# A hybrid attention and Fourier encoder layer on one core: where the meta rows' sums are stored, where the last sums of a weight are made, and which cast comes first in the merge

## The chip, the cores and the metric

The kernel runs on one core of one Trainium2 chip. The core has a matrix engine (TensorE, PE in the profile, with its weight loads as PEld), a vector engine (VectorE, DVE), a scalar engine (ScalarE, ACT), a general engine (GpSimd, POOL) and an engine that only issues transfers (SyncE, SP). Each works through its own list of instructions in order, and semaphores tie the lists together. Transfers between the main memory (HBM) and the on-chip memory (SBUF) run on 16 DMA engines; a transfer is issued from the list of one engine, here from SP's or POOL's. TensorE writes into eight banks of a separate memory, PSUM. The metric is the device time of one execution in microseconds (us); lower is better.

## The reference, cut to what matters

Two request groups go through one layer with the same weights: a sample of 512 positions and a prompt of 1024. Sixteen learned meta tokens stand in front of each. For the change these lines matter:

```python
x = jnp.concatenate([meta, x], axis=1)                       # 16 meta rows first
h = rmsnorm(x, g_mix)
q, k, v, u, gate_na, gate_fn = split(h @ w_in)
y_na = neighbourhood_attention(q, k, v, rel_bias, meta_bias) @ w_branch_na
f = jnp.fft.fft2(u, axes=(positions, group channels), norm='ortho').real
y_fn = f @ w_branch_fn
mixed = sigmoid(gate_na) * y_na + sigmoid(gate_fn) * y_fn
x = x + mixed @ w_out
a = relu(rmsnorm(x, g_mlp) @ w_up)
x = x + (a * a) @ w_down
y = rmsnorm(x, g_final)[16:]                                 # meta rows dropped
```

All arithmetic is float32.

## The kernel before, in words

**Numbers in two parts.** Every operand of a matmul is held as a high part (a rounded copy, cast by ScalarE, `L152` or `L133`) and a low part (the rest, subtracted by POOL or VectorE, `L153` or `L134`). A product is three matmuls (`mm3`, L129): high by high, high by low, low by high. A weight tile thus costs a load into a raw buffer, a cast and a subtraction (`weights`, L146 to L156) before TensorE can use it. The raw buffers of `wtile` are two, so the third weight of a stream is loaded when the first has been subtracted.

**Order.** The sample goes first through the whole layer up to the MLP, then the prompt, which takes the down projection of both. The kernel is traced as one long program; a planner in the compiler orders each engine's list by the order of the trace and by estimated times. The kernel holds it back by hand in two ways: `behind(marks)` puts every instruction of a block behind given instructions of the same engine, and `pinned()` puts it behind the last instruction that has been traced on each engine. So what is pinned keeps its place in the list of its engine, and a transfer that waits holds up everything behind it on SP.

**The sample's stages around the change.**
- `project_v` (L306 on) makes the values and stores them; it also sees the normed, transposed activations `hT` with the meta columns in front, and runs once with `meta is None`, for the sample.
- `gates` (L774 on) makes the two sigmoid gates of eight blocks `dm`, 24 matmuls each. Between its steps it advances two generators: `fold_u`, and then `fold_positions` (L863 on), the latter eight times. A step of `fold_positions` adds high and low parts of `hT` into a buffer `a` (for the sample one buffer, the tile `gain` of pool `mlp`) and into another `b`, stores the first 16 columns of `a` to `hmeta` in HBM (L885), and folds `a` and `b` onto each other (L886 to L888). `hmeta` is read once, by the prompt (L411).
- `merge_na` (L808 on) multiplies the attention's output with W_na and the gate. It is behind the marks of `gates` at `dm == 5`. Its weights are loaded at L813 into the tile `relu`.
- `fn_ahead` (L835 on) is a generator. W_fn is needed as eight tiles, each the sum or difference of two inputs A and B (L845, two VectorE instructions a tile, called a sum below; there are eight sums). A goes into one of four buffers `raw`, B into one of the two halves of `gain`. The result is stored to HBM for the prompt (L847, `wfn`), and the first four are split at once into high and low parts. One call makes the sum of the tile asked for in the call before, and asks for the next tile (L853).
- `fourier_channels` (L955 on) is the transform over channels, in two parts of three position tiles. After each tile it calls `fn_ahead`, pinned: twice in part 0 and once in part 1 (L1000). With one call at the end of `merge_na` that makes ten, where nine are needed.
- `fourier_positions` (L1016 on) is the transform over positions. It needs the high and low parts of `uc` and `us` that the stage before has made; it ends on VectorE with L1054 and L1055.
- `merge_fn` (L903 on) multiplies with W_fn, gates and adds: on VectorE L938 (times the gate) and L939 (plus the attention's part) for each `dm`. After each second `dm` the pair is split, ScalarE L945 and VectorE L946, two instructions each. Behind this, pinned, a W_out tile is loaded, cast and subtracted (`out_weights`, L1059). The third W_out tile is subtracted by VectorE, the others by POOL.
- `project_out` (L1067 on) multiplies with W_out. Its first two products take the first three merged pairs and W_out tiles, and the fourth follows.

## Time and profile before

| | |
|---|---|
| three runs | 1954.2, 1959.82, 1959.96 us |
| their median | 1959.82 us |
| the profiled execution, its own time | 1960.86 us |
| its span, first to last instruction | 1959.0 us |
| mean granted clock of TensorE | 0.992 |
| TensorE busy | 1902.8 us, 97% |
| VectorE, ScalarE, GpSimd busy | 1151.1, 733.3, 815.0 us |
| mean rate of the transfers | 183 GB/s |

How to read it: the span is the time from the first to the last instruction of the one execution that was profiled, and the time of that execution is a little longer. A busy share is the share of the span in which an engine had an instruction under way; matmuls are pipelined, so a busy TensorE is not TensorE at its peak. The granted clock is the share of full speed that TensorE was given; it is shown for each stretch that one asks for. In a timeline a row stands for one instruction or for a run of like ones: start, duration, engine, line of the kernel, operation, output and input, shape, count, and in brackets how long the engine had been idle before and who ended that. The views are named in the prediction where their rows are shown.

### The profile page before, as it was taken

What the parts mean: (1) busy time and instruction counts of PE and PEld (TensorE: products, weight loads), DVE (VectorE), ACT (ScalarE), POOL (GpSimd) and SP (SyncE); (2) the same over time, 40 slices, a digit from 0 to 9 for tenths busy, and PEclk for the clock granted to TensorE, in tenths of its full rate; (3) what the DMA queues carried; (4) which work ended last, traced back from release to release, by engine and by line L of the source; (5) the groups of instructions that cost most, each with busy time, mean ns of one, the idle gap of its engine ahead of it and who ended that gap; (6) DMA issues with size and microseconds to landing.
All of it is one profiled execution on the core that took longest, in us unless ns stands there. A gap on an engine that the chain in (4) does not pass through costs nothing.

```text
span 1959.0 us, 26257 instructions
## 1 busy us (share of the span) xinstructions
PE 1902.8 (97%) x9435; PEld 1594.7 (81%) x9435; DVE 1151.1 (59%) x1916; ACT 733.3 (37%) x1292; POOL 815.0 (42%) x672
## 2 busy tenths in 40 slices
PE   7999999999999999999999999999999999999997
PEld 5888787888888888888898877888887888888886
DVE  6771744799625566660427475656665326758668
ACT  3664323344314556641223233333343323323333
POOL 1344535355521233333134217978882323323331
PEclk9999999999999999999999999999999999999999
DMA  6756873677756455374452432544446868558733
GB/s 218 198 146 214 220 224 97 201 246 252 248 191 186 124 153 144 113 238 113 114 158 81 172 97 86 183 172 160 174 163 238 293 213 291 205 202 303 260 103 124
DMA packets 313058, 358.39 MB, mean 183 GB/s; under 512 B 51880, under 2 KB 222504, under 8 KB 312376
## 3 DMA queue, kind: packets, MB, share of 16 engines
q1 hardware_dynamic: 295168, 334.93, 52.0%
q0 software_dynamic: 17760, 21.80, 4.9%
q8 instruction: 74, 1.21, 0.3%
q14 instruction: 56, 0.46, 0.1%
HBM read 263.06 MB, written 96.16 MB: 183 GB/s over the span
## 4 chain that ended last, share of the span: by engine, by line
PE 74%; DVE 8%; DMA 6%; issue 5%; POOL 3%; ACT 3%; SPq 1%; DVEq 0%; ACTq 0%; POOLq 0%
PE ps_mm L129 19%; PE ps_o L129 17%; PE ps_s L129 15%; PE ps_t L129 10%; PE ps_mm L522 3%; PE ps_mm L523 3%; PE ps_mm L524 3%; POOL w_lo L153 2%; PE ps_o L671 2%; PE ps_t L651 1%; DVE st L182 1%; DMA w_raw<-in_w_in 1%; DMA hmeta<-gain 1%; DMA w_raw<-in_w_out 1%; DVE h_lo L153 1%
## 5 line engine op out<-in xcount | busy, mean ns | idle before, releaser
L153 POOL TENSOR_TENSOR w_lo<-w_raw,w_hi 128x1024 fp32r<-128x1024 f32 x71 | 179.2, 2524 | 226.7 <-ACT w_hi L152 175.9
L153 POOL TENSOR_TENSOR w_lo<-raw,w_hi 128x1024 fp32r<-128x1024 f32 (+1 forms) x49 | 101.4, 2073 | 213.5 <-ACT w_hi L152 206.9
L152 ACT CAST w_hi<-w_raw 128x1024 fp32r<-128x1024 f32 x88 | 92.5, 1051 | 172.9 <-PE ps_s L129 48.9
L153 DVE TENSOR_TENSOR h_lo<-long,h_hi 128x1024 fp32r<-128x1024 f32 x54 | 84.6, 1569 | 79.1 <-ACT h_hi L152 79.1
L522 PE MATMUL ps_mm<-hT,w_hi 128*128 128x512 f32 (+2 forms) x296 | 122.0, 412 | 0.0
L523 PE MATMUL ps_mm<-hT,w_hi 128*128 128x512 f32 (+2 forms) x296 | 111.0, 375 | 0.0
L524 PE MATMUL ps_mm<-hT,w_lo 128*128 128x512 f32 (+2 forms) x296 | 110.9, 375 | 0.0
L152 ACT CAST h_hi<-long 128x1024 fp32r<-128x1024 f32 x54 | 56.7, 1050 | 106.6 <-issue 31.0
L153 DVE TENSOR_TENSOR hs_lo<-short,hs_hi 128x512 fp32r<-128x512 f32 x54 | 63.8, 1182 | 41.9 <-ACT hs_hi L152 41.8
L645 ACT ACTIVATE sc<-sc,ast 128x288 f32<-128x288 f32 (+4 forms) x96 | 53.9, 561 | 71.2 <-DVE ast L643 71.0
L1380 POOL TENSOR_TENSOR x<-w_hi,x 128x512 fp32r<-128x512 f32 (+1 forms) x42 | 70.9, 1688 | 16.3 <-ACT x L1383 16.3
L152 ACT CAST w_hi<-raw 128x1024 fp32r<-128x1024 f32 (+1 forms) x49 | 40.9, 840 | 89.5 <-DVE raw L1596 51.8
L671 PEld LDWEIGHTS ps_o<-pt,vb 104*64 104x64 f32 (+6 forms) x576 | 62.9, 164 | 10.8 <-POOL vb L608 2.6
L671 PE MATMUL ps_o<-pt,vb 104*64 104x128 f32 (+6 forms) x576 | 62.5, 244 | 2.9 <-POOL vb L608 1.2
L524 PEld LDWEIGHTS ps_mm<-hT,w_lo 128*128 128x128 f32 x296 | 56.0, 189 | 10.5
L129 PE MATMUL ps_t<-gate,x 128*128 128x512 f32 x264 | 63.7, 390 | 0.0
L608 POOL TENSOR_TENSOR vb<-vr,vb 96x384 fp32r<-96x384 f32 (+4 forms) x48 | 48.6, 1029 | 34.7 <-ACT vb L607 34.6
L129 PE MATMUL ps_mm<-gate,x 128*128 128x512 f32 x256 | 62.6, 389 | 0.0
L643 DVE CUSTOM_DVE_ANT_0 sc<-ps_s,bm 128x288 f32<-128x288 f32 (+4 forms) x96 | 46.3, 482 | 23.7 <-issue 10.7
L765 POOL MEMSET bm<- 64x96 f32 (+2 forms) x64 | 11.2, 175 | 116.2 <-DVE ast L643 96.1
L129 PEld LDWEIGHTS ps_t<-gate,x 128*128 128x128 f32 x264 | 49.4, 188 | 10.9 <-DVE r_lo L1493 0.7
L523 PEld LDWEIGHTS ps_mm<-hT,w_hi 128*128 128x128 f32 x296 | 56.5, 191 | 1.6
(686 smaller groups left out, 5597.0 us busy)
## 6 DMA issues: line engine op xcount, KB each, us to landing
long<-hidden_prompt SPq DMA_DIRECT2D x54, 512.0 KB
w_raw<-in_w_in SPq DMA_DIRECT2D x52, 512.0 KB
raw<-in_w_down SPq DMA_DIRECT2D x39, 512.0 KB
w_raw<-in_w_up SPq DMA_DIRECT2D x34, 512.0 KB
hidden_prompt<-h SPq DMA_DIRECT2D x32, 512.0 KB
short<-hidden_sample SPq DMA_DIRECT2D x54, 256.0 KB
w_lo<-in_w_down SPq DMA_DIRECT2D x18, 512.0 KB
w_raw<-in_w_out SPq DMA_DIRECT2D x16, 512.0 KB
```

Of the source, the lines that this page charges most:

```text
L129: self.nc.tensor.matmul(out, a, b, start=(i == 0 and not more), stop=(i == len(terms) - 1), skip_group_check=more)
L152: nc.scalar.copy(out=hi, in_=raw)
L153: (lo_engine or nc.gpsimd).tensor_tensor(out=lo, in0=raw, in1=hi.bitcast(F32), op=ALU.subtract)
L182: nc.vector.scalar_tensor_tensor(out=a, in0=y, scalar=y, in1=v, op0=ALU.mult, op1=ALU.mult)
L522: nc.tensor.matmul(ps, a[0], b[0], start=(kt == 0), stop=False)
L523: nc.tensor.matmul(ps, a[0], b[1], start=False, stop=False)
L524: nc.tensor.matmul(ps, a[1], b[0], start=False, stop=(kt == 7))
L608: nc.gpsimd.tensor_tensor(out=lo, in0=vs, in1=hi.bitcast(F32), op=ALU.subtract)
L643: nc.vector.tensor_tensor_reduce(out=sc[:, :W], in0=ps[:, :W], in1=bm[:, :W], scale=1.0, scalar=3e38, op0=ALU.add, op1=ALU.min, accum_out= ...
L645: nc.scalar.activation(out=sc[:, :W], in_=sc[:, :W], func=AF.Exp, bias=st[:, 0:1], scale=-1.0, accum_out=st[:, 1:2])
L671: nc.tensor.matmul(po[:m, j * 128:(j + 1) * 128], v, x, start=(i == 0), stop=(i == len(ops) - 1))
L1380: self.nc.gpsimd.tensor_tensor(out=to, in0=x, in1=y, op=op)
```

## The change

- In `project_v`, when it runs for the sample, the high and low parts of the sixteen meta columns of `hT` are added for all eight blocks at once, into a tile of the values' pool (`pt0`), and stored to `hmeta` with one transfer. The eight stores in `fold_positions` are gone.
- `fn_ahead` asks for tiles one call earlier: the first call asks for two, each further one for one more. `fourier_channels` calls it twice a tile in part 0 and not in part 1. The calls that are left make the last two sums; they run, pinned, after `fourier_positions`.
- In `merge_fn`, at up to 512 positions, the W_out tile is taken (loaded, cast, subtracted; pinned) in front of the split of the merged pair, not behind it. At 1024 positions the order stays.

```diff
@@ project_v
             else:
                 nc.sync.dma_start(self.vd[64 + t * 128:64 + (t + 1) * 128], vs)
+        if meta is None:
+            hm = p.tile([128, 512], F32R, name="pt0", tag="pt0", bufs=self.ptb).bitcast(F32)[:, :8 * NM].rearrange("p (k m) -> p k m", k=8)
+            nc.vector.tensor_tensor(out=hm, in0=hT[0][:, :, 0:NM].bitcast(F32), in1=hT[1][:, :, 0:NM].bitcast(F32), op=ALU.add)
+            nc.sync.dma_start(self.hmeta.rearrange("k p c -> p k c"), hm)
@@ run, behind the Fourier stage
+            with self.pinned():
+                for _ in ahead:
+                    pass
             if not small:
                 close_sin()
@@ fn_ahead
         other = other()
+        raw = []
         for dm in range(9):
             if dm:
-                a, b = raw
+                a, b = raw.pop(0)
                 for s, op in ((slice(0, 2), ALU.add), (slice(2, 4), ALU.subtract)):
                     nc.vector.tensor_tensor(out=a[:, s], in0=a[:, s], in1=b[:, s], op=op)
                 self.wfn.append(self.dram.tile([128, 4, 128], F32, name=f"wfn{dm}"))
                 nc.sync.dma_start(self.wfn[-1], a)
                 self.fn_ready.append(self.fn_weights(p, dm - 1, a) if dm <= 4 else a)
+            for to in range(dm + 1 if dm else 0, min(dm + 2, 8)):
+                raw.append((p.tile([128, 4, 128], F32, name="raw", bufs=4),
+                            other[:, to % 2 * 512:(to % 2 + 1) * 512].rearrange("p (a b) -> p a b", a=4)))
+                for i in range(2):
+                    nc.sync.dma_start(raw[-1][i], self.rows(("w_fnA", "w_fnB")[i], to * 128))
             if dm < 8:
-                raw = (p.tile([128, 4, 128], F32, name="raw", bufs=4),
-                       other[:, dm % 2 * 512:(dm % 2 + 1) * 512].rearrange("p (a b) -> p a b", a=4))
-                for i in range(2):
-                    nc.sync.dma_start(raw[i], self.rows(("w_fnA", "w_fnB")[i], dm * 128))
                 yield
@@ fold_positions
-            if not m:
-                nc.sync.dma_start(self.hmeta[kt], a[:, 0:NM])
@@ merge_fn
             if dm % 2:
+                early = T <= 512
+                if early:
+                    with self.behind(split), self.pinned():
+                        self.wo.append(next(wout))
                 m.append((gate(), gate()))
                 for i in range(2):
                     nc.scalar.copy(out=m[-1][0][:, i], in_=total[i])
                     nc.vector.tensor_tensor(out=m[-1][1][:, i], in0=total[i], in1=m[-1][0][:, i].bitcast(F32), op=ALU.subtract)
 
-                with self.behind(split), self.pinned():
-                    self.wo.append(next(wout))
+                if not early:
+                    with self.behind(split), self.pinned():
+                        self.wo.append(next(wout))
@@ fourier_channels
-                    for _ in range(2 - part):
+                    for _ in range(0 if part else 2):
                         with self.pinned():
                             next(ahead, None)
```

## The prediction

> **What bounds the kernel now.** I read the page's busy times first, then who TensorE waits for in the stage that the change touches (the waits, PE alone, 200 to 340 us), then the granted clock around those waits (the windows), and last the timelines of the other engines, one engine at a time.

> ```profile
> PE 1902.8 (97%) x9435; PEld 1594.7 (81%) x9435; DVE 1151.1 (59%) x1916; ACT 733.3 (37%) x1292; POOL 815.0 (42%) x672
> ```

> ```profile
> PE ps_s L129 <- DVE us L134: 3.4, 2, 1.9
> PE ps_s L129 <- ACT w_hi L152: 2.7, 1, 2.7
> PE ps_o L129 <- DVE wo_lo L153: 1.1, 1, 1.1
> PE ps_o L129 <- ACT wo_hi L152: 1.1, 1, 1.1
> ```

> ```profile
> 222.90:230.10 7.20, 7.20 (x25) 5.79 (x26) 6.99 (x5) 3.09 (x5) 6.88 (x6) 0.76 0.49 121
> 279.20:288.40 9.20, 7.28 (x33) 6.51 (x34) 3.46 (x9) 1.57 (x4) 1.99 (x2) 0.81 0.70 233
> 309.98:319.50 9.52, 8.43 (x29) 6.55 (x30) 4.73 (x7) 3.14 (x4) 3.85 (x2) 0.82 0.24 59
> ```

> TensorE is busy for 97% of the span (columns of the second view: who waits, for whom, microseconds in all, times, the longest). So only time in which it stands still, or runs below full clock, can be won. In the sample half's gates, Fourier and merge stages it stands still in exactly three places, for 2.7, 3.4 and 1.1 + 1.1 = 2.2 us, together 8.3 us. Behind each the granted clock (the third column from the right) falls. Lost time there is (1 - clock) x window: 0.24 x 7.20, 0.19 x 9.20 and 0.18 x 9.52, which is 1.7 us each time. So the three places cost 4.4, 5.1 and 3.9 us, 13.4 in all; call them A, B and C. The chain of waits shows the clock's share directly at A: the group of 24 matmuls behind the stall takes 7.36 us, the same group after it 5.44.

> ```profile
> 222.86 7.36 PE ps_s L129 x24
> 230.22 5.44 PE ps_o L129 x24
> ```

> [...]

> **Part 1, the meta rows (stall A).** SP's timeline, one row of VectorE's and two of ScalarE's:

> ```profile
> 206.63 0.38 SPq L269 DMA_DIRECT2D wu<-w_lo  x1
> 207.37 9.25 SPq L885 DMA_DIRECT2D hmeta<-gain  x2
> 216.67 0.43 SPq L813 DMA_DIRECT2D relu<-in_w_na  x1
> ```

> ```profile
> 213.68 2.59 DVE L883 TENSOR_TENSOR gain<-hT,hT 128x264 f32<-128x264 f32 x1 [4.72 <-DMA hmeta<-gain]
> ```

> ```profile
> 221.25 0.62 ACT L152 CAST hid_hi<-relu 128x512 fp32r<-128x512 f32 x1 [11.29 <-DMA relu<-in_w_na]
> 221.77 1.04 ACT L152 CAST w_hi<-w_raw 128x1024 fp32r<-128x1024 f32 x1
> ```

> Each of the eight fold steps writes the one `gain` buffer, stores its first 16 columns as `hmeta`, and the next step may not write the buffer before that store has landed (4.72 us of VectorE's idle time at 213.68). The fourth store waits on SP for that step, until about 216.3, and W_na's first load stands behind it, since merge_na is held behind the gates of dm 5. Its cast at 221.25 heads ScalarE's queue; the gate weights' cast at 221.77 stands behind it, and TensorE waits for that. The change removes all eight stores and their WAR wait. W_na's load then goes out behind the store at 206.63, nine microseconds sooner, and the ScalarE queue is free when TensorE's previous group ends. A goes whole: -4.4 us. What is late next is the weights' own load, which had been in the buffer for long when the cast ran.

> What it adds: one add of 128 x 128 elements and one 64 KB store in project_v.

> ```profile
> 51.61 0.42 DVE L567 TENSOR_TENSOR k<-ps_o,k 64x256 fp32r<-64x256 f32 x1 [3.33 <-ACT k L565]
> ```

> ```profile
> L885 SPq DMA_DIRECT2D hmeta<-gain x8: 319/338/826, 197.3 to 235.6; - x8
> ```

> The add (at most the 0.42 us of this row, for fewer elements) falls into the 3.33 us in which VectorE waits for the keys. The store costs SP one issue of 0.34 us ahead of the value spread, which waits for the last value store anyway. Without that cover it is 0.3 to 0.8 us once; I take 0. The store's 64-byte pieces are the same as eight small stores had, moved to 50 us.

> **Part 2, the sums of W_fn (stall B).** VectorE through the end of the Fourier stage, and the ScalarE cast of the last sine part:

> ```profile
> 275.29 0.76 DVE L845 TENSOR_TENSOR raw<-raw,gain 128x256 f32<-128x256 f32 x2 [1.30 <-DMA gain<-in_w_fnB]
> 275.96 0.41 DVE L134 TENSOR_TENSOR us<-ps_o,us 128x252 fp32r<-128x252 f32 x1
> 277.60 1.25 DVE L845 TENSOR_TENSOR raw<-raw,gain 128x256 f32<-128x256 f32 x2 [1.23 <-DMA raw<-in_w_fnA]
> 278.77 0.41 DVE L134 TENSOR_TENSOR us<-ps_mm,us 128x252 fp32r<-128x252 f32 x1
> 280.49 0.76 DVE L845 TENSOR_TENSOR raw<-raw,gain 128x256 f32<-128x256 f32 x2 [1.32 <-DMA gain<-in_w_fnB]
> 281.17 0.40 DVE L134 TENSOR_TENSOR us<-ps_s,us 7x252 fp32r<-7x252 f32 x1
> ```

> ```profile
> 274.40 0.36 ACT L133 CAST us<-ps_s 7x252 fp32r<-7x252 f32 x1 [2.37 <-PE ps_s L129]
> ```

> All three high parts of `us` exist by 274.8, but the low parts leave VectorE at 276.4, 279.2 and 281.6, because sums 7 and 8 (277.60 and 280.49), each waiting for a load, stand between them. With these two moved behind the Fourier stage the three subtractions follow sum 6 at once: 276.4, 276.8, 277.2. TensorE used the second at 279.2 and the third at 281.6, so it gets each at least 2.4 us sooner, and both before it would have got there. B goes: -5.1 us. Sums 1 to 6 keep their place; if their loads, two deep through the two halves of one tile, came later against TensorE than here, each microsecond is one of B. The bound from below is a B that keeps the wait of sum 6 and wins about 2 us.

> The two sums go to VectorE behind the transform's last subtraction:

> ```profile
> 286.22 0.49 DVE L1055 SCALAR_TENSOR_TENSOR fT<-fs,sgn,fT 128x263 fp32r<-128x263 f32 x1
> 290.14 0.69 DVE L938 TENSOR_TENSOR gate<-ps_mm,gate 128x512 f32<-128x512 f32 x1 [3.43 <-PE ps_mm L129]
> ```

> There VectorE waits 3.43 us for TensorE; the sums take 2 x 0.76 = 1.5. Cost 0 while both loads have landed: with B gone VectorE comes there at 286.7 - 5.1 = 281.6 of the old times, and sum 8 had its load by 280.5. But SP's queue is moved too:

> ```profile
> 278.88 2.75 SPq L847 DMA_DIRECT2D wfn<-raw  x2
> 281.71 0.38 SPq L166 DMA_DIRECT2D gain<-in_g_mlp  x1
> 282.20 43.64 SPq L146 DMA_DIRECT2D w_raw<-in_w_out  x8
> ```

> The W_out loads are pinned behind the last of the sums' stores, and the load of `gain` needs the buffer of the last sum. In this time frame (the end of the Fourier matmuls held where it was) sum 8 ends at about 288.2, and W_out's first load is asked for at about 289 instead of 282.2.

> **Part 3, W_out in front of the merged casts (stall C).**

> ```profile
> 307.12 0.69 DVE L939 TENSOR_TENSOR hn<-gate 128x512 f32<-128x512 f32 x1
> ```

> ```profile
> 310.31 1.21 DVE L153 TENSOR_TENSOR wo_lo<-w_raw,wo_hi 128x1024 fp32r<-128x1024 f32 x1
> ```

> ```profile
> 307.84 1.14 ACT L945 CAST gate<-hn 128x512 fp32r<-128x512 f32 x2 [4.43 <-DVE hn L939]
> 308.89 1.04 ACT L152 CAST wo_hi<-w_raw 128x1024 fp32r<-128x1024 f32 x1
> ```

> ScalarE stands idle before 307.84 and then casts the merged pair first and the third W_out tile second; VectorE makes that tile's low part at 310.31, and TensorE waits once for each. In the new order the cast runs in the idle time, and the low part follows the sum at 307.8, ending at 309.0. The merged pair itself is not sooner: its sum still ends at 307.8. So C can go whole (-3.9) only if the merge's VectorE chain is no later than now. Against that stands the late first load. A W_out load took 4.04 us in the chain of waits:

> ```profile
> 320.42 4.04 DMA w_raw<-in_w_out
> ```

> Asked for at 289, with the second one and `gain` behind it, it lands between 293.0 (alone) and 297 (sharing, twice that). Its cast (1.05) is now in front of the first merged cast:

> ```profile
> 294.46 1.15 ACT L945 CAST gate<-hn 128x512 fp32r<-128x512 f32 x2 [3.02 <-DVE hn L939]
> ```

> That cast and VectorE's chain behind it are thus delayed by 0 to 3.6 us. I take 1.0, nearer the lone row, since only these few transfers are in flight: C gives -2.9, between 0 and -3.9.

> **Give-back.** The chain of W_out and W_up loads through two raw buffers starts at W_out and is not helped as much as TensorE. In project_out the norm's ScalarE pass already stands behind such a cast:

> ```profile
> 339.59 1.05 ACT L152 CAST w_hi<-w_raw 128x1024 fp32r<-128x1024 f32 x1 [6.30 <-DMA w_raw<-in_w_up]
> 340.55 1.05 ACT L174 ACTIVATE relu<-acc 128x1024 bf16<-128x1024 f32 x1
> ```

> If that cast stays where it is while TensorE comes 3 us sooner, the norm loses up to 3; I take +1.0. Nothing in the prompt half is edited: its generator is empty and `early` is false at 1024 positions.

> **Sum.** -4.4 - 5.1 - 2.9 + 1.0 = -11.4. Against the profiled execution, 1960.86 us, that is 1949.5; the median of the runs, 1959.82, is 1.0 below it, so 1948.5.

> **The rivals.** [...] POOL and VectorE block each other:

> ```profile
> 296.63 2.40 POOL L153 TENSOR_TENSOR w_lo<-w_raw,w_hi 128x1024 fp32r<-128x1024 f32 x1 [2.76 <-ACT w_hi L152]
> ```

> ```profile
> 297.05 2.54 DVE L939 TENSOR_TENSOR hn<-gate 128x512 f32<-128x512 f32 x1
> ```

> The add at 297.05 took 2.54 us instead of the 0.69 at 307.12, ending just behind the POOL subtraction. W_out's POOL subtractions now come sooner, amid the merge, the fourth too. Two more such meetings, 1.9 us each, use up all of C: -4.4 - 5.1 + 1.0 = -8.5, 1951.3. [...] For it: the add at 307.12 runs undisturbed now, with POOL's W_out work before and after it. Against: the number of tiles is the same, so a meeting that comes at one place goes at another. Chance 0.15.

> *The change does half of what it says.* Sum 6 still ends at 276.05 in front of the low parts; if the planner puts more in front of them, or the loads slip against a TensorE that comes 4.4 us sooner, B gives 0 to 2: -4.4 - 1 - 2.9 + 1 = -7.3 at best, with a C that also fails -4.4, 1952.5 to 1955.4. Chance 0.18, of which 0.05 faster. That new orders elsewhere give all of it back, near 1959: 0.07.

> *Slower.* Sums 7 and 8 now head VectorE's queue in front of the whole merge, and SP's in front of W_out. If their loads land late, VectorE's 3.4 us of cover are gone, and from there each microsecond of lateness moves the whole merge, and W_out's loads with it. To end 0.3% slower it must eat the 11.4 and 5.9 more, a landing over 20 us after the Fourier stage. Loads there keep VectorE waiting 1.2 to 1.3 us. Chance 0.08, 1966 or more.

> **How the numbers follow.** The forecast case has 0.52, 1946 to 1951. About 0.3%, 5.9 us, is what a measurement of this kernel can tell from no change. Faster: 0.52 + 0.15 + 0.05 = 0.72. Same: 0.13 + 0.07 = 0.20. Slower: 0.08. The range goes down to 1942: the full 13.4 (1946.4) and most of the 5.6 us by which the lowest of the three runs lies under their median. It goes up to 1958, over the half-done case.

> **What would show it.** Right: no wait of TensorE for `w_hi` near 220, nor for `us` in the Fourier stage; full clock there; W_na's first load about 9 us sooner; sums 7 and 8 directly before the first L938; W_out's third cast before the merged pair's. Wrong: a merged cast waiting behind W_out's load, a VectorE add stretched to 2 us beside POOL near 309 to 313, or TensorE waiting on `gate` in project_out instead of on `wo`.

## The result, and the profile after

| kernel | median | runs | ratio to the kernel before, 95% interval |
|---|---|---|---|
| before, on the same chip | 1958.56 us | 5 (1954.2 to 1959.96) | |
| changed | 1946.88 us | 5 (1946.61 to 1949.49) | 0.9946 [0.9933, 0.9959] |
| changed, on another chip (before there: 1958.76 us) | 1947.41 us | 5 (1943.87 to 1948.29) | 0.9936 [0.9924, 0.9947] |

The change makes the kernel faster by 8 to 13 us in 1958.6. The forecast was 1948.5 us. One execution of the kernel before, in the experiments, took 5077.09 us; it counts in no ratio and no mean. The profiled execution of the changed kernel took 1946.61 us, with a span of 1944.8; it was 1960.86 and 1959.0 before.

First the busy times on the page of the changed kernel. TensorE's work is the same 9435 matmuls; its busy time fell by 4.6 us, because half-clock matmuls count as busy too (the group of 24 behind A took 7.36 us before and takes 5.44 now).

```profile
PE 1898.2 (98%) x9435; PEld 1592.6 (82%) x9435; DVE 1150.8 (59%) x1917; ACT 733.5 (38%) x1292; POOL 813.8 (42%) x672
```

Next, who TensorE waits for between 150 and 340 us (columns as in the prediction), and the windows of that stage (the clock is the third column from the right):

```profile
PE ps_s L129 <- POOL w_lo L153: 1.3, 1, 1.3
PE ps_o L129 <- ACT gate L956: 0.4, 1, 0.4
```

```profile
195.00:240.00 45.00, 45.00 (x204) 37.45 (x203) 35.70 (x61) 17.87 (x39) 27.38 (x22) 1.00 0.96 273
240.00:270.00 30.00, 30.00 (x215) 26.94 (x215) 10.90 (x32) 6.91 (x17) 11.62 (x17) 1.00 0.67 196
270.00:300.00 30.00, 29.59 (x138) 24.39 (x138) 25.72 (x33) 11.58 (x19) 17.20 (x10) 1.00 0.52 165
300.00:330.00 30.00, 30.00 (x134) 24.74 (x133) 9.06 (x20) 8.30 (x10) 14.36 (x6) 1.00 0.32 95
```

The waits for `w_hi`, `us`, `wo_lo` and `wo_hi` are gone; of 8.3 us a wait of 0.4 is left, for the merged pair. (The 1.3 us for `w_lo` lie at 158 us, ahead of the change; they were 1.4 before.) From 195 to 330 us TensorE is busy for 134.6 of 135 us at full clock.

The three mechanisms, one engine at a time. SP:

```profile
189.87 0.58 SPq L820 DMA_DIRECT2D relu<-in_w_na  x1
...
270.20 0.52 SPq L146 DMA_DIRECT2D w_raw<-in_w_out  x1
275.21 1.05 SPq L855 DMA_DIRECT2D wfn<-raw  x2
276.36 0.41 SPq L146 DMA_DIRECT2D w_raw<-in_w_out  x1
276.86 0.46 SPq L166 DMA_DIRECT2D gain<-in_g_mlp  x1
```

W_na's first load goes out at 189.87 instead of 216.67, which is 27 us sooner and not the nine of the prediction: without the stores it stands elsewhere in SP's list. W_out's first load (270.20) stands in front of the last two sums' stores (275.21), not behind them. VectorE:

```profile
268.50 0.76 DVE L853 TENSOR_TENSOR raw<-raw,gain 128x256 f32<-128x256 f32 x2 [1.29 <-DMA gain<-in_w_fnB]
269.18 0.42 DVE L134 TENSOR_TENSOR us<-ps_o,us 128x252 fp32r<-128x252 f32 x1
269.51 0.41 DVE L134 TENSOR_TENSOR us<-ps_mm,us 128x252 fp32r<-128x252 f32 x1
269.84 0.40 DVE L134 TENSOR_TENSOR us<-ps_s,us 7x252 fp32r<-7x252 f32 x1
...
274.44 1.46 DVE L853 TENSOR_TENSOR raw<-raw,gain 128x256 f32<-128x256 f32 x4
277.33 0.69 DVE L945 TENSOR_TENSOR gate<-ps_mm,gate 128x512 f32<-128x512 f32 x1 [1.44 <-PE ps_mm L129]
```

The three low parts of `us` follow sum 6 without a break. Sums 7 and 8 (the four instructions at 274.44) end in front of the first product of the merge, and VectorE still waits 1.44 us for TensorE there. ScalarE in the gates and in the merge:

```profile
217.15 1.36 ACT L152 CAST hid_hi<-relu 128x512 fp32r<-128x512 f32 x2 [4.64 <-DMA relu<-in_w_na]
218.41 1.04 ACT L152 CAST w_hi<-w_raw 128x1024 fp32r<-128x1024 f32 x1
...
276.10 1.05 ACT L152 CAST w_hi<-w_raw 128x1024 fp32r<-128x1024 f32 x1 [2.68 <-DMA w_raw<-in_w_out]
...
281.92 1.14 ACT L956 CAST gate<-hn 128x512 fp32r<-128x512 f32 x2 [3.28 <-DVE hn L946]
...
284.96 1.04 ACT L152 CAST wo_hi<-w_raw 128x1024 fp32r<-128x1024 f32 x1
288.83 1.14 ACT L956 CAST gate<-hn 128x512 fp32r<-128x512 f32 x2 [2.83 <-DVE hn L946]
290.41 1.06 ACT L152 CAST wo_hi<-w_raw 128x1024 fp32r<-128x1024 f32 x1 [0.43 <-DMA w_raw<-in_w_out]
295.85 1.14 ACT L956 CAST gate<-hn 128x512 fp32r<-128x512 f32 x2 [4.38 <-DVE hn L946]
```

ScalarE still waits 4.64 us for two of W_na's loads in front of a cast of gate weights, but that cast ends at 219.45 and TensorE begins the group that needs it at 222.59, without a wait. W_out's first cast (276.10) is long done when the first merged cast comes (281.92). Its third (284.96) precedes even the second merged cast (288.83), and its fourth (290.41) the third (295.85).

Set against each other matmul by matmul (the k-th of 9435 in both traces), the lead of the changed kernel grows by 4.6 us over the gates, 5.3 over the Fourier stage and 3.3 over the merge, and shrinks by 0.6 in project_out. At the start of the gates it is already 3.1 us, 1.7 of it at 145 us where neither kernel differs in its work, and at 790 us, again in equal work, it loses 1.6. In the traces each of the two is one stretch of 3.413 us at clock 0.50, at 144.98 us in the kernel before and at 789.11 us in the changed one; such a stretch is called a half-clock window below.

### The profile page after: what moved, and what is told of

Read it like the earlier page. It is cut to its first block, busy times and chain, and to the rows that moved or that the text cites. A ratio compares the mean times of both kernels' runs of the same rounds, so it can differ in the third digit from the quotient of the medians.

```text
span 1944.8 us, 26239 instructions
## 1 busy us (share of the span) xinstructions
PE 1898.2 (98%) x9435; PEld 1592.6 (82%) x9435; DVE 1150.8 (59%) x1917; ACT 733.5 (38%) x1292; POOL 813.8 (42%) x672
## 3 DMA queue, kind: packets, MB, share of 16 engines
q8 instruction: 74, 1.21, 0.3%
## 4 chain that ended last, share of the span: by engine, by line
PE 80%; DVE 8%; DMA 5%; issue 3%; ACT 3%; POOL 2%; SPq 1%; ACTq 0%; DVEq 0%; POOLq 0%
PE ps_mm L129 21%; PE ps_o L129 19%; PE ps_s L129 16%; PE ps_t L129 10%; PE ps_mm L529 3%; PE ps_mm L530 2%; PE ps_mm L531 2%; PE ps_o L678 2%; PE ps_t L658 1%; DVE st L182 1%; POOL w_lo L153 1%; DVE h_lo L153 1%; DMA w_raw<-in_w_up 1%; DMA w_raw<-in_w_out 1%; DMA r<-in_x_prompt 1%
## 5 line engine op out<-in xcount | busy, mean ns | idle before, releaser
L153 POOL TENSOR_TENSOR w_lo<-w_raw,w_hi 128x1024 fp32r<-128x1024 f32 x71 | 177.1, 2494 | 228.0 <-ACT w_hi L152 182.2
L153 POOL TENSOR_TENSOR w_lo<-raw,w_hi 128x1024 fp32r<-128x1024 f32 (+1 forms) x49 | 101.3, 2070 | 211.6 <-ACT w_hi L152 205.7
L152 ACT CAST w_hi<-w_raw 128x1024 fp32r<-128x1024 f32 x88 | 92.4, 1050 | 177.2 <-PE ps_s L129 49.8
L153 DVE TENSOR_TENSOR h_lo<-long,h_hi 128x1024 fp32r<-128x1024 f32 x54 | 84.6, 1568 | 79.2 <-ACT h_hi L152 78.0
L152 ACT CAST h_hi<-long 128x1024 fp32r<-128x1024 f32 x54 | 56.7, 1049 | 106.5 <-PE ps_s L129 30.0
L153 DVE TENSOR_TENSOR hs_lo<-short,hs_hi 128x512 fp32r<-128x512 f32 x54 | 63.1, 1168 | 42.5 <-ACT hs_hi L152 42.5
L152 ACT CAST w_hi<-raw 128x1024 fp32r<-128x1024 f32 (+1 forms) x49 | 40.9, 839 | 88.5 <-DVE raw L1608 51.9
L129 PE MATMUL ps_t<-gate,x 128*128 128x512 f32 x264 | 63.7, 391 | 0.0
L129 PE MATMUL ps_mm<-gate,x 128*128 128x512 f32 x256 | 62.6, 390 | 0.0
L129 PEld LDWEIGHTS ps_t<-gate,x 128*128 128x128 f32 x264 | 49.4, 188 | 11.0 <-DVE r_lo L1505 0.8
```

Source lines behind the costliest of these rows:

```text
L129: self.nc.tensor.matmul(out, a, b, start=(i == 0 and not more), stop=(i == len(terms) - 1), skip_group_check=more)
L152: nc.scalar.copy(out=hi, in_=raw)
L153: (lo_engine or nc.gpsimd).tensor_tensor(out=lo, in0=raw, in1=hi.bitcast(F32), op=ALU.subtract)
```

## The experiments

Unless another is named, each edit is made to the kernel before. In the table of the parts "less" is worked out as (1 - ratio) x 1958.6 us, with the interval in brackets; a ratio compares runs on the same chip. The median of the kernel before was 1958.33 us on the chip of e1 to e4, 1959.41 on that of e5 to e8 and 1958.76 on that of e9 to e12.

### Each part alone, and each part left out

The hunks of the change, one at a time (`e1_meta`, `e2_sums`, `e3_wout`), and the changed kernel with one of them undone (`e4_no_wout`, `e5_no_sums`, `e6_no_meta`):

```diff
 part 1   +            nc.sync.dma_start(self.hmeta.rearrange("k p c -> p k c"), hm)
          -                nc.sync.dma_start(self.hmeta[kt], a[:, 0:NM])
 part 2   +                for _ in ahead:
          +                    pass
          -                    for _ in range(2 - part):
          +                    for _ in range(0 if part else 2):
 part 3   +                if early:
          +                    with self.behind(split), self.pinned():
          +                        self.wo.append(next(wout))
```

> Part 1 alone on the kernel before. Theory (each stall costs its idle time and a half-clock window behind it): 4.4 to 4.6 us less, no wait of TensorE for w_hi near 220, clock 1.00 there. Rival (idle time alone counts, the clock window comes by chance and turns up elsewhere): 2.7 us less. Rival (stall A only moves to the next load): under 1 us less, with a new wait in the same stage.

> Part 2 alone on the kernel before. Theory: both waits for us go with their window, 5.1 to 5.3 us less; W_out's first load stands in front of the last two stores on SP, as in the changed kernel. Rival (idle time alone): 3.4 us less. Rival (the low parts get stuck behind sum 6, or the two sums stand in the way of the merge): 0 to 2 us less.

> Part 3 alone on the kernel before: W_out's loads are issued where they were, only the order of the casts is new. Theory (stall C goes without any help of part 2): 3.3 to 3.9 us less. Rival (idle time alone): 2.2 us less. Rival (VectorE and GpSimd meet more often in the merge, or the cast delays the merged pair): 0 to 1 us less, with TensorE waiting for gate or wo_lo near 310.

> Parts 1 and 2 without part 3. Theory (the three parts add up, each with its own price): 9.7 us less than before, and the wait for wo_hi and wo_lo in project_out is still there, about 2.2 us, with a clock window behind it. Rival (part 3's gain came with part 2, whose merge starts earlier against W_out's loads): 12 us or more less than before and no such wait.

> Parts 1 and 3 without part 2. Theory (the parts add up): 7.7 to 8.2 us less than before, both waits for us still there, 3.4 us. Rival (with part 1 TensorE comes 4.4 us sooner and waits longer for sums 7 and 8): 4 to 6 us less than before, waits for us of 5 us or more.

> Parts 2 and 3 without part 1. Theory (the parts add up): 8.4 to 8.7 us less than before, the wait for w_hi of 2.7 us and its window still there. Rival (idle time alone counts): 5.6 us less than before.

| kernel | median | less than before | waits of TensorE at A, B, C in its profile |
|---|---|---|---|
| e1_meta (part 1) | 1954.57 us | 2.7 us [0.8, 4.7] | 0, 3.4, 1.1 + 1.1 |
| e2_sums (part 2) | 1953.68 us | 5.1 us [2.7, 7.2] | 2.3, 0, 1.1 + 1.1 |
| e3_wout (part 3) | 1955.16 us | 0.6 us [-2.0, 3.1] | 2.2, 3.3, 1.1 |
| e4_no_wout (1 and 2) | 1949.85 us | 7.4 us [4.7, 10.2] | 0, 0.5, 1.1 + 1.1 |
| e5_no_sums (1 and 3) | 1952.41 us | 5.5 us [3.3, 7.6] | 0, 3.3, 0 |
| e6_no_meta (2 and 3) | 1949.12 us | 8.2 us [5.5, 10.8] | 2.3, 0, 0.2 |

Each part takes away its own wait and leaves the others, but part 3 alone leaves 1.1 us of C, now for the merged pair. (e2_sums and e6_no_meta also wait 0.8 us in all for W_na's own high parts, near 250 us.) TensorE's waits between 300 and 340 us there:

```profile
PE ps_o L129 <- ACT gate L949: 1.1, 1, 1.1
```

Why the merged pair comes late in e3_wout can be read from ScalarE and VectorE:

```profile
301.51 1.05 ACT L152 CAST wo_hi<-w_raw 128x1024 fp32r<-128x1024 f32 x1 [4.63 <-DMA w_raw<-in_w_out]
302.47 1.14 ACT L949 CAST gate<-hn 128x512 fp32r<-128x512 f32 x2
```

```profile
303.12 3.08 DVE L950 TENSOR_TENSOR gate<-hn,gate 128x512 fp32r<-128x512 f32 x2 [1.51 <-ACT gate L949]
```

The fourth W_out tile's cast waits for its load and stands in front of the second merged cast, whose sum was done at 301.60. GpSimd's subtraction of that tile begins at 302.64, and VectorE's split of the pair, 1.29 us when undisturbed, lasts 3.08. In the changed kernel that tile is cast behind the second merged pair. No run changed this order alone.

The times fit the size of part 2 (its idle time alone, 3.4, lies inside the interval too), and of part 1 as idle time (2.7) rather than as 4.4, though 4.4 lies inside its interval. Two expectations lie outside: 3.3 to 3.9 for part 3 alone, and 7.7 to 8.2 for e5_no_sums, just above 7.6; the rival there, waits for `us` of 5 us or more, did not come either. For part 3 one run of 1965.51 us weighs much: the mean of all eleven is 1.1 us under that of the kernel before, and without it 2.0. The three parts alone add up to 8.4 us, all three together gave 10.6 and 12.5; with intervals of 2 us and more for each, the times don't settle whether they add up. The rival that the idle time alone counts is not settled by these times either. The traces say more. At A, e2_sums, e3_wout and e6_no_meta waited 2.2 to 2.3 us for `w_hi`, and in none of them did the clock fall. First the row in e6_no_meta, then the six microseconds behind it (clock 1.00); the last fence is the same stretch in the kernel before (0.72):

```profile
219.48 3.92 PE L129 MATMUL ps_s<-hT,w_hi 128*128 128x512 f32 x16 [2.26 <-ACT w_hi L152]
```

```profile
219.48:225.48 6.00, 6.00 (x26) 4.99 (x27) 5.07 (x4) 3.13 (x5) 5.68 (x5) 1.00 0.50 130
```

```profile
222.86:228.86 6.00, 6.00 (x19) 4.82 (x20) 5.75 (x5) 3.13 (x5) 5.68 (x5) 0.72 0.43 105
```

C's 1.1 + 1.1 us cost a half-clock window in the kernel before and in e2_sums, and none in e1_meta, e4_no_wout and e7_own_place (below). B's 3.3 to 3.4 us cost one in the kernel before, e3_wout and e5_no_sums, and two in e1_meta. So the same wait costs 1.7 us of clock in one execution and nothing in the next. The next experiment measures which pauses have a half-clock window behind them.

### Pauses of a known length

`e9_gaps` does none of the reference's work: it leaves everything out but matmuls of 512 columns on loaded data, in 100 groups, with a pause between two groups.

```diff
+            for step in LADDER:                      # 256 to 3584 columns
+                m = 36 + (7 * n) % 23
+                for i in range(m):
+                    nc.tensor.matmul(ps, wt, hot[:, 0:512], start=(i == 0), stop=(i == m - 1))
+                for k, c in enumerate(step):
+                    if k == 0:
+                        nc.scalar.copy(out=hot[:, 0:1], in_=ps[:, 0:1])
+                    nc.scalar.copy(out=hot[:, 0:c], in_=raw[:, 0:c])
```

> Not the reference's work: 100 groups of 36 to 58 matmuls of 512 columns, and between two groups a pause of TensorE that lasts as long as ScalarE copies 256 to 3584 columns, ten lengths from about 1 to 4 us, ten times each. Theory (the clock is judged in fixed windows of 3.41 us, and a window in which TensorE stands still for about half of it or more halves the next one): no half window behind pauses under 1.5 us; behind pauses of 2 to 3 us one in a part of the cases, about pause over 3.41 of them; behind pauses over 3.5 us always one. Rival (a pause of 3.4 us or more is needed, shorter ones cost nothing): half windows behind the two longest pauses only. Rival (every pause over 2.5 us costs one, shorter ones none, wherever the windows lie): all or none for each length.

| pause, us | 0.7 | 1.0 | 1.4 | 1.8 | 2.0 | 2.5 to 2.7 | 2.9 | 3.1 | 3.5 | 4.2 |
|---|---|---|---|---|---|---|---|---|---|---|
| pauses | 10 | 10 | 10 | 10 | 10 | 10 | 10 | 10 | 10 | 9 |
| with a half-clock window behind | 0 | 0 | 0 | 5 | 4 | 5 | 9 | 6 | 9 | 9 |

Two pauses of 2.03 us in TensorE's timeline, and two windows of 4 us that begin where these two pauses end:

```profile
67.42 12.80 PE L32 MATMUL ps<-hot,wt 128*128 128x512 f32 x48 [2.03 <-ACT hot L37]
```

```profile
491.53 8.69 PE L32 MATMUL ps<-hot,wt 128*128 128x512 f32 x37 [2.03 <-ACT hot L37]
```

```profile
67.42:71.42 4.00, 4.00 (x11) 3.12 (x12) 0.00 (x0) 0.00 (x0) 0.00 (x0) 0.57 0.00 0
491.53:495.53 4.00, 4.00 (x18) 3.31 (x19) 0.00 (x0) 0.00 (x0) 0.00 (x0) 1.00 0.00 0
```

Equal pauses, clock 0.57 and 1.00. But for the last, behind the last matmul, all half-clock stretches of this run are one or two times 3.413 us long, and they begin on one grid of 3.413 us. So it is in the traces of the two kernels. In the kernel before, the stretches ahead of the last begin at 144.98, 223.48, 281.51, 312.23, 1168.97 and 1503.48 us, the last five 23, 40, 49, 300 and 398 times 3.413 us behind the first (to 0.04 of a step); the one at 1168.97 is 6.827 us long, the others 3.413. In the changed one they begin at 789.11, 1154.33 and 1488.84 us, 107 and 205 steps behind the first. Cutting the pauses of e9 by its grid, in windows of 3.413 us: of 43 windows that held 1.95 us of a pause or more, all were followed by a half-clock window; of nine with 1.80 to 1.95, five; with less, only windows that ran at half clock themselves. So in this run a pause cost 1.7 us (3.413 at half clock) if more than about 1.9 us of it fell into one window. A pause of 2 to 3.5 us was split by a grid line or not, which is chance: the first theory fits these counts, with 1.9 of 3.413 us for its "about half", and both rivals fall. (Its "always" over 3.5 us missed one of ten, a pause of 3.53 us.) How the clock is set no trace shows; that it is judged in these windows is the author's reading of the counts.

The traces of the kernels, cut by their own grids, settle A, B and C. At these places each window with 1.97 us or more of standstill was followed by a half-clock window, and none with 1.53 or less. In the kernel before the fullest windows at A, B and C held 2.66, 2.90 and 2.16 us. A grid line splits the wait at A into 0.90 and 1.35 in e2_sums, 1.07 and 1.15 in e3_wout, 1.48 and 0.78 in e6_no_meta, and C's two waits of 1.1 fall into two windows in e1_meta, e4_no_wout and e7_own_place. Elsewhere in these traces windows with 1.55 to 1.93 us went either way (in the kernel before, 1.56 us at 141.57 with clock 0.50 behind it, and 1.75 us at 359.99 with 1.00), so these counts give no sharp bound.

In the kernels the spread goes with the clock. Of the 65 runs of the kernel before beside the experiments, on three chips, those with a mean clock of 0.991 took 1961.9 us on average, with 0.992, 0.993 and 0.994 they took 1959.7, 1958.5 and 1957.1, and with 0.996 (two runs) 1953.2. It is the same program each time.

### What held W_na's load at A

Two kernels. `e7_own_place` keeps the eight stores, each from a copy in one of two small places. `e10_idle_stores` is the changed kernel with eight transfers of the same size, written at the old places in the program, which wait for nothing.

```diff
 e7   -                nc.sync.dma_start(self.hmeta[kt], a[:, 0:NM])
      +                own = self.zero48[:, 8 + kt % 2 * 16:24 + kt % 2 * 16]
      +                nc.vector.tensor_copy(own, a[:, 0:NM])
      +                nc.sync.dma_start(self.hmeta[kt], own)
 e10  +                nc.sync.dma_start(self.spare[kt], self.hmeta[kt])
```

> The kernel before with all eight stores kept in their places of SP's queue, but each from a copy of its 16 columns in one of two places of their own, so that a fold step never waits for a store of the buffer it writes. It takes away the wait on the store alone. Theory of the prediction (the fold step that waits for the store holds SP's queue and so W_na's load): stall A goes whole or nearly, 3.5 to 4.5 us less. Rival (the stores' places in SP's queue hold W_na's load, whatever the buffer): 0 to 1 us less.

> The changed kernel with eight transfers of the size of the old meta stores, DRAM to DRAM, at the fold steps' places in SP's queue; they wait for nothing of the fold. Theory (what cost at stall A was that a store in SP's queue waits for a fold step, not that it stands there): within 1 us of the changed kernel, no wait of TensorE for w_hi near 220. Rival (eight more entries of SP's queue, 0.3 to 0.5 us each, and their small pieces are enough): the wait is back with 2 us or more, 3 to 4.5 us more than the changed kernel.

`e7_own_place`: 1961.36 us against 1959.41, ratio 1.0014 [1.0002, 1.0026], so slower by 0.4 to 5.1 us; stall A is 4.3 us. The theory's number failed. VectorE's and SP's timelines show why:

```profile
214.28 2.70 DVE L887 COPY zero<-gain 128x16 f32<-128x16 f32 x1 [4.61 <-DMA hmeta<-zero]
...
218.51 3.75 DVE L891 TENSOR_TENSOR acc<-gain,acc 128x263 f32<-128x263 f32 x1
```

```profile
217.00 0.34 SPq L888 DMA_DIRECT2D hmeta<-zero  x1
...
223.19 0.34 SPq L888 DMA_DIRECT2D hmeta<-zero  x1
223.64 0.37 SPq L814 DMA_DIRECT2D relu<-in_w_na  x1
224.95 0.34 SPq L888 DMA_DIRECT2D hmeta<-zero  x1
225.40 0.38 SPq L814 DMA_DIRECT2D relu<-in_w_na  x1
```

With two places the fifth copy waits for a landing (4.61 us), so the wait was put off, not taken away. Then VectorE steps that take 0.17 and 0.43 us elsewhere in this trace last 2.70 and 3.75 beside POOL's subtractions (2.41 us from 213.68, 2.79 for two from 216.83, 2.39 from 219.59). The stores stay behind these steps on SP, and W_na's third and fourth loads behind the stores, at 223.64 and 225.40; the cast of the fourth is the one in front of the `w_hi` that TensorE waits for. `e10_idle_stores`: 1947.29 us, ratio 0.9936 [0.9923, 0.9949], the same as the changed kernel's 0.9936 on that chip; between 200 and 340 us TensorE waits for nothing but 0.3 us for a merged pair. Eight entries in SP's queue cost nothing that shows; in the kernel before, and in e7_own_place, the entries that wait for a VectorE step stand in front of the late loads. In e10_idle_stores W_na's first load also went out early, at 191.09, in front of seven of the eight entries, so the wait alone, with the old order on SP, is not tested. A kernel with the eight stores and no wait on a landing at all was not tried.

### W_out's first load behind the sums' stores

`e8_late_load` is the changed kernel with the order on SP that the prediction had assumed:

```diff
+            sums_done = self.mark((mybir.EngineType.SP,))
-                    with self.behind(split), self.pinned():
+                    with self.behind(split), self.behind(sums_done), self.pinned():
```

> The changed kernel with W_out's first load held on SP behind the stores of sums 7 and 8, as the prediction had taken it to be. Prediction's step: the load goes out some 6 us later than in the changed kernel, its cast holds the first merged cast, and the time is 1.0 us more than the changed kernel (0 to 3.6). Rival (the idle time of ScalarE in front of the first merged cast, 3.3 us in the changed kernel, hides it): within 0.3 us of the changed kernel. Rival (both buffers are late, and the wait for wo_hi comes back): 3 us or more.

It took 1948.14 us, ratio 0.9952 [0.9936, 0.9968]; the changed kernel's two ratios, 0.9946 and 0.9936, lie within. In its profile the load goes out at 278.60, its cast now stands directly in front of the first merged cast, and the wait for a merged pair is 1.0 us (0.4 and 0 in the two profiles of the changed kernel):

```profile
277.50 1.01 SPq L856 DMA_DIRECT2D wfn<-raw  x2
278.60 0.96 SPq L146 DMA_DIRECT2D w_raw<-in_w_out  x2
```

```profile
283.14 1.05 ACT L152 CAST w_hi<-w_raw 128x1024 fp32r<-128x1024 f32 x1 [2.18 <-DMA w_raw<-in_w_out]
284.09 1.14 ACT L957 CAST gate<-hn 128x512 fp32r<-128x512 f32 x2
```

But that cast holds nothing: the first merged sum ends at 283.95 and the merged cast begins at 284.09, 0.1 us later. What is new stands on VectorE and GpSimd, first in e8_late_load, then VectorE's same step in the changed kernel:

```profile
280.95 3.00 DVE L947 TENSOR_TENSOR hn<-gate 128x512 f32<-128x512 f32 x2
...
284.74 5.28 DVE L958 TENSOR_TENSOR gate<-hn,gate 128x512 fp32r<-128x512 f32 x2 [0.19 <-ACT gate L957]
```

```profile
284.27 2.41 POOL L153 TENSOR_TENSOR w_lo<-w_raw,w_hi 128x1024 fp32r<-128x1024 f32 x1 [0.87 <-ACT w_hi L152]
```

```profile
282.58 1.61 DVE L957 TENSOR_TENSOR gate<-hn,gate 128x512 fp32r<-128x512 f32 x2 [0.69 <-ACT gate L956]
```

GpSimd subtracts the late tile, and the next one right behind it, just when VectorE splits the first merged pair, and the split lasts 5.28 us instead of 1.61. So the late load costs 0.6 to 1.0 us of idle time, near the 1.0 that the prediction charged, but by these rows through that meeting and not through a held cast: the first rival was right about the cast. The time alone can't tell the cost from none.

### A version that should be faster still

What is left near there is a wait of 1.8 us for the last low part in project_out, where a norm step of VectorE is held by POOL. `e11_up_later` holds the cast of the tile that POOL subtracts then:

```diff
+                with self.layer.behind(self.turned if f == 3 else []):
+                    self.w[f] = self.layer.weights(self.layer.rows("w_up", f * 128), to)
...
+        mlp.turned = self.mark((mybir.EngineType.Activation,))
```

> The changed kernel with the cast of W_up's fourth tile held behind the third first step of the MLP, so that GpSimd's subtraction of 2.36 us at 344 no longer holds VectorE's norm step (2.34 instead of 0.22 us) in front of the low part that TensorE waits for. Theory: the wait for gate of 1.8 us at 345 falls to 0.3 or less, 1.5 to 2.4 us less than the changed kernel. Rival (the subtraction meets another VectorE instruction later, or the tile comes late): within 0.5 us of the changed kernel, with a wait for another low part behind 355.

> The changed kernel itself, on the same chip as the two versions of it above. Every theory: 10 to 12 us less than the kernel before. Theory of the windows: the spread of its own runs goes in steps of about 1.7 us with the mean clock, without any new wait.

1950.13 us, ratio 0.9955 [0.9943, 0.9967], against 0.9936 [0.9924, 0.9947] for the changed kernel on the same chip: no gain. TensorE's waits between 335 and 400 us in e11_up_later and, below, between 340 and 400 in the changed kernel:

```profile
PE ps_t L194 <- DVE r L184: 4.4, 1, 4.4
PE ps_s L129 <- DVE gate L134: 0.6, 1, 0.6
```

```profile
PE ps_s L129 <- DVE gate L134: 2.0, 2, 1.8
```

The wait fell from 1.8 to 0.6 and a wait of 4.4 took its place: the held cast keeps its raw buffer, W_up's next load goes out later, and the prompt's norm, which must be done for the transposes at 393, is late. The rival was right in kind, a tile that comes late, but not in where it shows or in its "within 0.5 us": the medians lie 2.7 us apart, with intervals that just overlap. `e12_after` is in the table at the top; its profile has no wait of TensorE between 200 and 340 us.

## Why the prediction was right, step by step

- **Bound.** Right: taking three waits away, 8.3 us of idle time, moved the time by 11.5 us on the mean of the runs (1958.5 for the 65 beside the experiments, 1947.0 for 10 of the changed kernel).
- **Part 1, A.** Right in what held TensorE: the load went out sooner and the wait for `w_hi` is gone whenever the stores are (e1, e4, e5). Its new place was not foreseen (27 us sooner, not nine). Its add (0.28 us) and store cost nothing that shows. e10 shows that eight entries on SP are not enough to bring A back; that the wait for the fold step is what counts fits the rows of the kernel before and of e7, with the old order on SP not tested alone.
- **Part 2, B.** Right: the low parts follow sum 6, the wait is gone in every kernel with part 2 (0.5 left in e4), and sums 7 and 8 end before the merge. VectorE's 1.44 us of wait behind them show that they cost nothing there.
- **Part 3, C: the step that failed.** "The W_out loads are pinned behind the last of the sums' stores" is false. The load is pinned behind the last entry traced on SP; that is the opening of the pool for W_out's tiles, which issues nothing. The load went out 5 us before the stores, its cast was hidden, and C gave 3.3, not 2.9. The price of 1.0 failed with it: with the assumed order (e8) the merged cast is held by 0.1 us, and by its rows the idle time comes from GpSimd's subtractions beside VectorE's split; that it comes near 1.0 is luck. What the prediction did not see: alone, part 3 leaves 1.1 us of C (e3), with parts 1 or 2 it leaves 0 to 0.4. In e3 a W_out cast that waits for its load holds the second merged pair.
- **Give-back.** Taken at 1.0, measured 0.6 in the profiles, at the place named: W_up's cast stands in front of the norm's pass on ScalarE. TensorE comes to project_out 16.1 us sooner than before, the norm's pass (340.55 then, 324.96 now) 15.6, and TensorE waits 0.3 us for a low part at 341.79 that it did not wait for before.

```profile
324.00 1.05 ACT L152 CAST w_hi<-w_raw 128x1024 fp32r<-128x1024 f32 x1 [6.29 <-DMA w_raw<-in_w_up]
324.96 1.06 ACT L174 ACTIVATE relu<-acc 128x1024 bf16<-128x1024 f32 x1
```

- **The clock's share, a term mis-sized.** The prediction added 1.7 us to each stall as if each brought one half-clock window every time. That was so in the profiled execution. The mean clock rose from 0.9929 to 0.9945 over the runs: (0.0071 x 1957) - (0.0055 x 1945) = 3.2 us of clock won, not 5.1. With the 8.3 us of idle time that makes the 11.5; the 0.4 left at C and the 0.6 given back are below what these means can tell. That the forecast's total came out so near is in part luck: the 1.9 us too much of clock stood against 1.0 for a late load and 0.4 of give-back that were charged and not paid.
- **Short pauses and the clock.** A wait of 2.7 us cost clock in the kernel before (0.76 over the 7.20 us behind it), and so did five of ten pauses of 1.8 us in e9. There the place of a pause on the grid of 3.413 us went with its price, and its length alone did not: of two pauses of 2.03 us one had clock 0.57 behind it and one 1.00.
- **The rivals.** Meetings of VectorE and GpSimd did not take all of C, but they have a part in what is left. In the merge the add at 291.73 lasts 2.75 us (0.69 at 307.12 in the kernel before), and VectorE works without a break from it to the third merged sum, for which TensorE waits 0.4 us. In e3 and e8 such meetings (3.08 and 5.28 us) stand in front of waits of 1.1 and 1.0. That is the wait for `gate` in project_out which the prediction had named as a sign of being wrong; it takes 0.4 of C's 2.2 us at most in the changed kernel. Sum 6 did not hold the low parts. Sums 7 and 8 were not late.

```profile
291.73 2.75 DVE L946 TENSOR_TENSOR hn<-gate 128x512 f32<-128x512 f32 x1
```

## What to carry to other kernels

A store that waited for a slow step held the loads behind it on SP here (two stores stood there for 9.25 us, and W_na's first load went out at 216.67 instead of 189.87); move the store, or make it wait for nothing. Eight entries that wait for nothing cost nothing here (1947.29 us with them, 1947.41 without). A stall of TensorE of 2 to 3.5 us is to be priced at its idle time plus a chance of 1.7 us, not plus 1.7 us (33 of 50 such pauses in e9 had a half-clock window behind them), and one profile shows only one draw of that chance. Before trusting an order written in the program, look in the engine's own list at what the load is really tied to. A wait that is as long as predicted can still have another cause; look for it in the rows in front of it.

## What the hardware showed that was not expected

```profile
344.23 2.34 DVE L182 SCALAR_TENSOR_TENSOR st<-st 128x1 f32<-128x1 f32 x1
```
